# A hybrid decoder trunk on one core: first queries earlier in attention's lead-in, compressed items spread, background reordered

## The chip, the cores and the metric

The kernel runs on one core of a Trainium2 chip. The metric is the device time of one execution in microseconds (us); lower is better. Before the change the median of three runs is 1143.22 us (1142.72 to 1144.98).

## The reference

The reference is a small two-layer decoder over one sequence of 512 tokens with 1024 features, in float32. Layer 0 is a gated short convolution and a squared-ReLU MLP of width 4096. Its output feeds one shared key/value side. Layer 1 is attention with 16 heads of 64 in 4 key/value groups, then a second MLP, then a final norm.

Attention is what the change concerns. For each group, queries attend in three branches:

- a **compressed** branch, over 31 tokens that a small MLP (`phi`) makes out of overlapping blocks of 32 raw keys or values;
- a **selected** branch, over the best blocks (here all causal blocks are taken, since 16 may be chosen and only 8 exist);
- a **window** branch over 512 tokens, which is all of the causal past.

Each branch is a softmax with a learned relative-position bias; three sigmoid gates weigh them, and an output projection adds the result to the residual:

```python
o = gt[..., 0:1] * o_c + gt[..., 1:2] * o_s + gt[..., 2:3] * o_w
...
return o.reshape(B, S, N_HEADS * HEAD_DIM) @ w_o
```

## The kernel before

**Number format.** Each float32 operand of a product is split into two float16 parts, high and low, and a product is three matmuls: high by high, low by high, high by low (`mm3`, L338, issues L339 to L341). Weights come as float32 pieces over SyncE's DMA queue (`load_piece`, L155 to L165). ScalarE makes the high part (L193), VectorE the low part (L194). Pieces are taken in the order of one list, `pieces`, written at the head of the kernel (L70 to L130), and are converted two ahead of their use.

**Attention's lead-in** (L865) runs six generators to their ends, one after the other: `keys(0)`, `keys(1)`, `values(0)`, `values(1)`, `gates()`, `queries(0)`. Key and query generators each issue 48 matmuls of 128x512 through `gated_pair` (L651). `queries(g)` (L730) then scales two banks on VectorE (L643), copies four 64-row heads to float16 on ScalarE (L738) and subtracts to get the low half on GpSimd (L739). A query tile `Q` has three buffers.

**Attention's main loop** (L1089 to L1107) walks a list of items. `Full(g, qb, br, heads)` (L917) is one 128-row query block of one branch, with up to 512 columns; a group has 22 of them. `Cmp(gp, qb)` (L990) is a query block of the compressed branch, for two groups at once; there are 8. Each item has five stages, and the loop runs stage 0 of item i, then stage 1 of item i-2, stage 2 of item i-3, stage 3 of item i-4 and stage 4 of item i-6:

- stage 0: query-key matmuls into one of two `b` banks (L937, L938; L1005, L1006 for `Cmp`), bias and minimum on VectorE (L945), exponential on ScalarE (L947);
- stage 1: transposes (L953; L1026) and the high half of the probabilities on ScalarE (L956);
- stage 2: the low half, `at_pl`, on VectorE (L959; L1033);
- stage 3: probability-value matmuls (L972 to L974; L1042 to L1044), scaling and adding of branches (`add_parts`, L872; VectorE L890, GpSimd L892 and L895);
- stage 4: `finish` (L897) transposes a finished block (L906) into `ot`.

The order of items is all of group 0, all of group 1, the four `Cmp(0, qb)`, group 2, the four `Cmp(1, qb)`, group 3. The items are numbered 0 to 95 below, so the `Cmp` are items 44 to 47 and 70 to 73, and groups 2 and 3 begin at items 48 and 74.

**Background.** Other matrix work is drawn in between, from one generator `background()` (L1073). `raw(w)` (L746) projects raw keys or values, rescales them with a strided read on VectorE (L757) and gathers them through twelve small DMAs on SyncE's queue into `big` (L763 to L765). `phi(w)` (L771) is the compressing MLP, 96 matmuls of 155 columns over `big`, with a short chain of small operations behind them (L798). `out_proj(0)` (L841) is the output projection of groups 0 and 1. The order is raw 0, queries 1, phi 0, raw 1, phi 1, queries 2, queries 3, then `out_proj(0)` once groups 0 and 1 are finished ("o1"). Each yield tells a price; after each item's stage 0 a credit is added (1.1 for items under 44, then 0.7), and background is drawn until the credit is spent. An item whose queries or compressed keys aren't there yet (`need`) first draws background until they are; such a draw isn't charged. After the loop, `out_proj(2)`, for groups 2 and 3, runs by itself, and the second MLP follows.

The written order is then arranged for each engine by the framework's scheduler, which may move instructions of different work past each other; each engine runs its own list strictly in that order.

Of the kernel before, what the change touches and what calls it, by code (L numbers as in the profile page):

```python
# [48 lines left out]
def body(ctx, tc, x, rel_bias, norm_mix, norm_mlp, mlp_w1, mlp_w2, a_w_in, a_conv_w, a_w_out,  # L49
# [50 lines left out]
    def block(w, c0, scale=SW, k0=0, kn=8):  # L100
        for k in range(k0, k0 + kn, 4):
            cols(w, c0, 256, scale, k, 4)
# [8 lines left out]
    for p in range(4):  # L111
        block(a_w_out[0], p * 256)
    mlp_pieces(0)
    for part in (2, 4, 3, 5):
        block(w_kv, part * 256)
    cols(b_w_qg[0], 1024, 48, SW)
    block(b_w_qg[0], 0)
    block(w_kv, 0)
    block(b_w_qg[0], 256)
    block(phi_k_w1, 0, SW, 0, 16)  # L120
    cols(phi_k_w2, 0, 64, SW, 0, 2)
    block(w_kv, 256)
    block(phi_v_w1, 0, SW, 0, 16)
    cols(phi_v_w2, 0, 64, SW, 0, 2)
    block(b_w_qg[0], 512)
    block(b_w_qg[0], 768)
    for g in range(0, 4, 2):
        for p in range(4):
# [75 lines left out]
    def next_piece():  # L204

        i = pos["use"]
        pos["use"] += 1
        while i not in ready:
            for _ in convert_piece():
                pass  # L210
        return ready.pop(i)
# [177 lines left out]
    for p in range(4):  # L389
        pc, pu, pb = [], [], []  # L390
        if p == 0:
# [10 lines left out]
            for c in range(6):  # L402
                w = next_piece()
# [194 lines left out]
    with pool("attn") as ap:  # L598
# [70 lines left out]
        def ahead_fine():  # L669
            while pos["cv"] < min(pos["use"] + AHEAD, len(pieces)):  # L670
                yield from convert_piece(512)
# [57 lines left out]

        def queries(g):  # L730
            po = yield from gated_pair(xq)
            q = ap.tile([128, 4, S], F16, name="Q", bufs=3)
            for m in range(2):
                t = scaled(po[m], rbq)
                for s in range(2):
                    h, r = 2 * m + s, slice(64 * s, 64 * s + 64)
                    o = slice(64 - 64 * s, 128 - 64 * s)
                    ACT.activation(q[r, h], t[r], AF.Copy)  # L738
                    POOL.tensor_tensor(q[o, h], t[r], q[r, h], op=OP.subtract)  # L739
                yield  # L740
            Qs[g] = q
# [96 lines left out]
        ss2 = SumSq()  # L838
        xm = None

        def out_proj(g):  # L841
            for p in range(4):
                w = next_piece()
                cv = ahead_fine()
                po = [abank(), abank()]
                for c in range(4):
                    for m in range(2):
                        mm3(po[m], [u[:, c, m * 128:(m + 1) * 128] for u in w], [u[:, 2 * g + c] for u in ot],
                            c == 0, c == 3)
                        next(cv, None)  # L850
                        yield 0.65
                for m in range(2):
                    residual_in(po[m], 2 * p + m, 1.0 / (SO * SW))
                    if g == 2:
                        ss2.add(X[:, 2 * p + m])
                if g == 2:
                    for m in range(2):
                        split_gain(xm, 2 * p + m, X[:, 2 * p + m], "mlp1")
                drain(cv)
# [2 lines left out]
            yield from gen  # L862
            done.add(name)

        for k in (keys(0), keys(1), values(0), values(1), gates(), marked("q0", queries(0))):  # L865
            drain(k)
        lead_in[0] = False

# [121 lines left out]
        class Cmp:  # L990
# [7 lines left out]

            def st0(self):
                gp, qb, n = self.gp, self.qb, self.n  # L1000
                s = bank("b")[:, 0:256].rearrange("p (h n) -> p h n", h=8)
                for j in range(8):
                    g, h = 2 * gp + j // 4, j % 4
# [62 lines left out]
        def full(g):  # L1066
            return [Full(g, qb, br, hs) for qb in range(4) for br in range(2) for hs in heads_of(qb)]

        items = full(0) + full(1) + [Cmp(0, qb) for qb in range(4)] + full(2) + [Cmp(1, qb) for qb in range(4)]
        items += full(3)  # L1070
        at_item = {11: lambda: load_T(1), 35: lambda: load_T(2), 60: lambda: load_T(3)}

        def background():  # L1073
            yield from raw(0)
            yield from marked("q1", queries(1))
            yield from phi(0)
            yield from raw(1)
            yield from marked("cmp", phi(1))
            yield from marked("q2", queries(2))
            yield from marked("q3", queries(3))  # L1080
            while "o1" not in done:
                yield "wait"
            yield from out_proj(0)
# [1 line left out]
        bg = background()  # L1085

        lead = {1: 2, 2: 3, 3: 4, 4: 6}
        credit = 0.0
        for i in range(len(items) + 6):  # L1089
            if i < len(items):  # L1090
                for k in items[i].need():
                    while k not in done:
                        if next(bg, "end") in ("wait", "end"):
                            raise RuntimeError(k)
                at_item.get(i, lambda: None)()
                items[i].st0()
            credit += 1.1 if i < 44 else 0.7
            while credit > 0.0:
                u = next(bg, "end")
                if u in ("wait", "end"):  # L1100
                    credit = 0.0
                else:
                    credit -= u or 0.1
            for s in (1, 2, 3, 4):
                j = i - lead[s]
                if 0 <= j < len(items):
                    getattr(items[j], f"st{s}")()  # L1107
# [1 line left out]
            pass  # L1109
        lead_in[0] = True  # L1110
        xm = new_split(work, "xs")
        drain(out_proj(2))
    xs = xm
    ss = ss2

# [140 lines left out]
```

## Time and profile before

| what | value |
|---|---|
| median of three runs | 1143.22 us |
| profiled execution | 1147.34 us |
| its span, first to last instruction | 1145.5 us |
| matmul engine (PE) busy | 1102.9 us, 96% |
| VectorE (DVE) busy | 833.8 us, 73% |
| ScalarE (ACT) busy | 569.7 us, 50% |
| GpSimd (POOL) busy | 152.8 us, 13% |
| mean granted clock of the matmul engine | 0.987 |

The profile counts a matmul as busy from its start to the end of its pipeline, so matmuls that follow each other overlap, and a busy share near 100% doesn't mean that no time is lost. Two other readings tell more: the idle time before an instruction with the instruction that ended it (written in brackets in the timeline), and the clock that the matmul engine was granted (PEclk, 1.00 is full speed). The times in the timeline count from the start of the span. Attention lies between about 507 us (first key matmul) and 807 us (last matmul of the output projection); the rest of the program is convolution and MLPs.

### The profile page before, as it was taken

How to read it: one execution, taken by the hardware profiler on the slowest of the kernel's cores; microseconds unless marked ns; L12 is line 12 of the kernel's file. 1: busy time of each engine (PE TensorE's matmuls, PEld its weight loads, DVE VectorE, ACT ScalarE, POOL GpSimd, SP SyncE). 2: the span in 40 equal slices, each digit the busy share in tenths (PEclk: the TensorE clock that was granted, in tenths of full speed). 3: DMA queues.
4: the chain of work that ended last, by engine and by line, in shares of the span. 5: the costliest groups of instructions: out<-in, count | busy, mean ns of one | idle time of the engine just before them, and what ended most of it. 6: DMA issues, size and time to landing. Idle time of an engine off the chain costs nothing.

```text
span 1145.5 us, 20148 instructions
## 1 busy us (share of the span) xinstructions
PE 1102.9 (96%) x7959; PEld 695.8 (61%) x7959; DVE 833.8 (73%) x1504; ACT 569.7 (50%) x925; POOL 152.8 (13%) x201
## 2 busy tenths in 40 slices
PE   8999999999999999999999889999999999999986
PEld 4444444447884458868467566665444788445875
DVE  5755557865897557987489878897885598754785
ACT  4523235445333444457669656776554533343452
POOL 0000000322000220000102003221122100122020
PEclk9999999999999999999899999999999999999998
DMA  6423235433333333314234241101633333330221
GB/s 208 130 92 110 93 111 166 122 95 97 125 100 109 110 110 100 104 45 131 93 77 132 75 152 38 39 20 56 198 115 111 96 111 112 108 94 17 77 89 74
DMA packets 149378, 115.75 MB, mean 101 GB/s; under 512 B 8612, under 2 KB 146564, under 8 KB 149284
## 3 DMA queue, kind: packets, MB, share of 16 engines
q1 hardware_dynamic: 146736, 109.47, 31.6%
q10 hardware_dynamic: 2260, 4.40, 1.3%
q8 instruction: 62, 1.02, 0.4%
q0 software_dynamic: 288, 0.61, 0.2%
q14 instruction: 32, 0.26, 0.1%
HBM read 110.22 MB, written 2.14 MB: 98 GB/s over the span
## 4 chain that ended last, share of the span: by engine, by line
PE 58%; DVE 17%; ACT 8%; issue 6%; POOL 5%; DMA 4%; SPq 0%; DVEq 0%; ACTq 0%; POOLq 0%
PE a L339 5%; PE a L340 5%; PE a L341 5%; POOL ml_z L501 4%; DMA wst<-mlp_w_dram 4%; PE c L341 3%; PE c L339 3%; PE c L340 3%; PE b L340 3%; PE b L339 3%; DVE wlo L183 3%; PE b L341 3%; ACT rh L502 3%; PE c L953 2%; DVE wlo L194 2%
## 5 line engine op out<-in xcount | busy, mean ns | idle before, releaser
L193 ACT ACTIVATE whi<-wst 128x1024 f16<-128x1024 f32 (+2 forms) x171 | 141.9, 856 | 133.8 <-PE b L340 39.3
L194 DVE SCALAR_TENSOR_TENSOR wlo<-wst,whi 128x1024 f16<-128x1024 f32 (+2 forms) x171 | 168.6, 992 | 53.6 <-ACT whi L193 53.2
L501 POOL TENSOR_TENSOR ml_z<-ml_z 128x256 f32<-128x256 f32 x128 | 95.7, 769 | 609.7 <-ACT ml_z L499 607.1
L182 ACT ACTIVATE whi<-wst 128x1792 f16<-128x1792 f32 x64 | 106.7, 1691 | 135.5 <-DVE wst L180 107.3
L339 PEld LDWEIGHTS <-whi 128*128 128x128 f16 x1024 | 100.7, 98 | 112.3 <-issue 4.2
L341 PEld LDWEIGHTS <-wlo 128*128 128x128 f16 x1024 | 100.5, 98 | 110.9 <-issue 1.5
L340 PEld LDWEIGHTS <-whi 128*128 128x128 f16 x1024 | 100.5, 98 | 108.2 <-issue 3.5
L503 DVE TENSOR_TENSOR rl<-ml_z,rh 128x1792 f16<-128x1792 f32 x32 | 64.8, 2026 | 130.7 <-ACT rh L502 130.6
L183 DVE SCALAR_TENSOR_TENSOR wlo<-wst,whi 128x1792 f16<-128x1792 f32 x64 | 128.8, 2019 | 3.3 <-ACT whi L182 2.9
L180 DVE TENSOR_TENSOR wst<-wst 128x256 f32<-128x256 f32 x256 | 110.1, 473 | 28.0 <-DMA wst<-mlp_w_dram 27.0
L502 ACT ACTIVATE rh<-ml_z 128x1792 f16<-128x1792 f32 x32 | 54.3, 1697 | 100.9 <-POOL ml_z L501 100.9
L549 PEld LDWEIGHTS <-whi 128*128 128x128 f16 x896 | 87.9, 98 | 15.3 <-issue 4.5
L550 PEld LDWEIGHTS <-wlo 128*128 128x128 f16 x896 | 87.9, 98 | 12.1 <-DVE wlo L183 1.0
L548 PEld LDWEIGHTS <-whi 128*128 128x128 f16 x896 | 88.0, 98 | 10.8
L947 ACT ACTIVATE at_p<-at_s,at_m 128x128 f32<-128x128 f32 (+3 forms) x128 | 70.9, 555 | 20.8 <-DVE at_m L945 20.2
L499 ACT ACTIVATE ml_z<-ml_t 128x1024 f32<-128x1024 f32 x32 | 33.8, 1057 | 93.1 <-DVE ml_t L497 93.1
L341 PE MATMUL b<-xsh,wlo 128*128 128x512 f16 x208 | 78.8, 379 | 0.0
L340 PE MATMUL b<-xsl,whi 128*128 128x512 f16 x208 | 78.8, 379 | 0.0
L339 PE MATMUL b<-xsh,whi 128*128 128x512 f16 x208 | 78.7, 379 | 0.0
L341 PE MATMUL c<-xsh,wlo 128*128 128x512 f16 x192 | 73.5, 383 | 0.0
L339 PE MATMUL c<-xsh,whi 128*128 128x512 f16 x192 | 73.5, 383 | 0.0
L340 PE MATMUL c<-xsl,whi 128*128 128x512 f16 x192 | 73.3, 382 | 0.0
(312 smaller groups left out, 2690.6 us busy)
## 6 DMA issues: line engine op xcount, KB each, us to landing
wst<-mlp_w_dram SPq DMA_DIRECT2D x256, 256.0 KB, 3.3
wst<-a_w_in_dram SPq DMA_DIRECT2D x18, 512.0 KB, 3.6
wst<-w_kv_dram SPq DMA_DIRECT2D x12, 512.0 KB, 3.6
T<-ext_d ACTq DMA_DIRECT2D x4, 1056.0 KB, 6.7
wst<-a_w_out_dram SPq DMA_DIRECT2D x8, 512.0 KB, 3.3
wst<-b_w_qg_dram SPq DMA_DIRECT2D x8, 512.0 KB, 4.1
wst<-b_w_o_dram SPq DMA_DIRECT2D x8, 512.0 KB, 3.3
wst<-a_w_in_dram SPq DMA_DIRECT2D x8, 384.0 KB, 5.6
```

Source lines behind the costliest of these rows:

```text
L180: DVE.tensor_tensor(b[:, :, o], b[:, :, x], b[:, :, y], op=e)
L182: ACT.activation(hi, b[:, :, 1:], AF.Copy, scale=sc)
L183: DVE.scalar_tensor_tensor(lo, b[:, :, 1:], sc, hi, op0=OP.mult, op1=OP.subtract)
L193: ACT.activation(hi[:, s:e], w, AF.Copy, scale=sc)
L194: DVE.scalar_tensor_tensor(lo[:, s:e], w, sc, hi[:, s:e], op0=OP.mult, op1=OP.subtract)
L339: PE.matmul(ps, w[0], xs[0], start=start, stop=False)
L340: PE.matmul(ps, w[0], xs[1], start=False, stop=False)
L341: PE.matmul(ps, w[1], xs[0], start=False, stop=stop)
L501: POOL.tensor_tensor(z[:, o], z[:, a], z[:, b], op=e)
L502: ACT.activation(rh[0][:, p], z[:, 1:8], AF.Copy)
L548: PE.matmul(acc7[i], wh, xh, start=c == 0 and not other, stop=False, skip_group_check=other)
L549: PE.matmul(acc7[i], wh, xl, start=False, stop=False, skip_group_check=other)
```

## The change

The change touches attention and the list of weight pieces that goes with it. In the lead-in, `queries(0)` comes third, ahead of `values(0)`, `values(1)` and `gates()`. In the background, `queries(2)` stands ahead of `phi(1)`. `queries(3)` waits, once its matmuls are drawn, until stage 0 of `Cmp(0, 3)` has been issued ("cmp0"), since it reuses the buffer of `Q` of group 0. The compressed items no longer stand four in a row: `Cmp(0, qb)` go among the last 12 items of group 2 (items 54, 57, 60 and 63), and `Cmp(1, qb)` among those of group 3 (items 74, 79, 84 and 89). Groups 2 and 3 therefore begin at items 44 and 70. The credit starts at 3.0, and an item adds 0.91 (items under 54), 0.72 (under 68) or 0.6. At the end, `out_proj(2, 2)` first issues, for two of its four column pieces, the products that need group 2 alone. The arithmetic is the same.

```diff
@@ -111,18 +111,20 @@
     for p in range(4):
         block(a_w_out[0], p * 256)
     mlp_pieces(0)
-    for part in (2, 4, 3, 5):
+    for part in (2, 4):
+        block(w_kv, part * 256)
+    block(b_w_qg[0], 0)
+    for part in (3, 5):
         block(w_kv, part * 256)
     cols(b_w_qg[0], 1024, 48, SW)
-    block(b_w_qg[0], 0)
     block(w_kv, 0)
     block(b_w_qg[0], 256)
     block(phi_k_w1, 0, SW, 0, 16)
     cols(phi_k_w2, 0, 64, SW, 0, 2)
     block(w_kv, 256)
+    block(b_w_qg[0], 512)
     block(phi_v_w1, 0, SW, 0, 16)
     cols(phi_v_w2, 0, 64, SW, 0, 2)
-    block(b_w_qg[0], 512)
     block(b_w_qg[0], 768)
     for g in range(0, 4, 2):
         for p in range(4):
@@ -729,6 +731,8 @@
 
         def queries(g):
             po = yield from gated_pair(xq)
+            while g == 3 and "cmp0" not in done:
+                yield "wait"
             q = ap.tile([128, 4, S], F16, name="Q", bufs=3)
             for m in range(2):
                 t = scaled(po[m], rbq)
@@ -838,17 +842,29 @@
         ss2 = SumSq()
         xm = None
 
-        def out_proj(g):
-            for p in range(4):
-                w = next_piece()
-                cv = ahead_fine()
-                po = [abank(), abank()]
-                for c in range(4):
+        def out_proj(g, early=0):
+
+            ws, pos_ = [], []
+
+            def products(p, chunks, cv=iter(())):
+                for c in chunks:
                     for m in range(2):
-                        mm3(po[m], [u[:, c, m * 128:(m + 1) * 128] for u in w], [u[:, 2 * g + c] for u in ot],
-                            c == 0, c == 3)
+                        mm3(pos_[p][m], [u[:, c, m * 128:(m + 1) * 128] for u in ws[p]],
+                            [u[:, 2 * g + c] for u in ot], c == 0, c == 3)
                         next(cv, None)
                         yield 0.65
+
+            for p in range(early):
+                ws.append(next_piece())
+                pos_.append([abank(), abank()])
+                drain(products(p, (0, 1)))
+            for p in range(4):
+                if p >= early:
+                    ws.append(next_piece())
+                    pos_.append([abank(), abank()])
+                po = pos_[p]
+                cv = ahead_fine()
+                yield from products(p, (2, 3) if p < early else range(4), cv)
                 for m in range(2):
                     residual_in(po[m], 2 * p + m, 1.0 / (SO * SW))
                     if g == 2:
@@ -862,7 +878,7 @@
             yield from gen
             done.add(name)
 
-        for k in (keys(0), keys(1), values(0), values(1), gates(), marked("q0", queries(0))):
+        for k in (keys(0), keys(1), marked("q0", queries(0)), values(0), values(1), gates()):
             drain(k)
         lead_in[0] = False
 
@@ -998,6 +1014,8 @@
 
             def st0(self):
                 gp, qb, n = self.gp, self.qb, self.n
+                if (gp, qb) == (0, 3):
+                    done.add("cmp0")
                 s = bank("b")[:, 0:256].rearrange("p (h n) -> p h n", h=8)
                 for j in range(8):
                     g, h = 2 * gp + j // 4, j % 4
@@ -1066,8 +1084,18 @@
         def full(g):
             return [Full(g, qb, br, hs) for qb in range(4) for br in range(2) for hs in heads_of(qb)]
 
-        items = full(0) + full(1) + [Cmp(0, qb) for qb in range(4)] + full(2) + [Cmp(1, qb) for qb in range(4)]
-        items += full(3)
+
+        def mixed(rest, cmps):
+            out_ = []
+            for i, item in enumerate(rest):
+                out_.append(item)
+                if i in cmps:
+                    out_.append(cmps[i])
+            return out_
+
+        items = full(0) + full(1)
+        items += mixed(full(2), {9 + 2 * qb: Cmp(0, qb) for qb in range(4)})
+        items += mixed(full(3), {3: Cmp(1, 0), 7: Cmp(1, 1), 11: Cmp(1, 3), 15: Cmp(1, 2)})
         at_item = {11: lambda: load_T(1), 35: lambda: load_T(2), 60: lambda: load_T(3)}
 
         def background():
@@ -1075,8 +1103,8 @@
             yield from marked("q1", queries(1))
             yield from phi(0)
             yield from raw(1)
+            yield from marked("q2", queries(2))
             yield from marked("cmp", phi(1))
-            yield from marked("q2", queries(2))
             yield from marked("q3", queries(3))
             while "o1" not in done:
                 yield "wait"
@@ -1085,7 +1113,7 @@
         bg = background()
 
         lead = {1: 2, 2: 3, 3: 4, 4: 6}
-        credit = 0.0
+        credit = 3.0
         for i in range(len(items) + 6):
             if i < len(items):
                 for k in items[i].need():
@@ -1094,7 +1122,7 @@
                             raise RuntimeError(k)
                 at_item.get(i, lambda: None)()
                 items[i].st0()
-            credit += 1.1 if i < 44 else 0.7
+            credit += 0.91 if i < 54 else 0.72 if i < 68 else 0.6
             while credit > 0.0:
                 u = next(bg, "end")
                 if u in ("wait", "end"):
@@ -1109,7 +1137,7 @@
             pass
         lead_in[0] = True
         xm = new_split(work, "xs")
-        drain(out_proj(2))
+        drain(out_proj(2, 2))
     xs = xm
     ss = ss2
```

## The prediction

> **What bounds the kernel now.** I read the page's totals first, then a table of stretches over attention alone, since every edit lies there, then the list of waits of the matmul engine (PE), and last the timeline at the places that the waits name.
>
> ```profile
> span 1145.5 us, 20148 instructions
> ...
> PE 1102.9 (96%) x7959; PEld 695.8 (61%) x7959; DVE 833.8 (73%) x1504; ACT 569.7 (50%) x925; POOL 152.8 (13%) x201
> ```
>
> The profiled execution took 1147.34 us, 1.8 us more than its span; the median is 1143.22 us. The sum below is made against the profiled execution and its saving carried over to the median. By busy time PE is the bound, but busy counts matmuls to the end of their pipeline, so the share hides losses. The stretches show where they are (busy us per engine, then clock).
>
> ```profile
> core 0: us, PE busy (x) PEld busy (x) DVE busy (x) ACT busy (x) POOL busy (x), PEclk, DMA share, GB/s
> 507.00:557.00 50.00, 50.00 (x417) 33.63 (x416) 36.67 (x72) 32.18 (x61) 0.03 (x1) 1.00 0.43 133
> 557.00:567.40 10.40, 7.98 (x36) 3.59 (x35) 4.38 (x22) 7.39 (x24) 4.94 (x4) 0.67 0.17 53
> ...
> 590.00:622.00 32.00, 30.41 (x372) 23.71 (x369) 27.95 (x82) 27.26 (x79) 5.77 (x5) 1.00 0.47 132
> ...
> 642.70:659.70 17.00, 12.30 (x151) 8.43 (x149) 13.89 (x30) 10.28 (x24) 0.99 (x2) 0.90 0.40 94
> 659.70:694.00 34.30, 29.27 (x313) 20.15 (x314) 25.21 (x80) 19.15 (x50) 7.37 (x8) 0.95 0.40 125
> 694.00:730.00 36.00, 34.49 (x351) 24.23 (x349) 31.79 (x88) 29.62 (x84) 11.03 (x10) 1.00 0.14 45
> 730.00:785.00 55.00, 54.57 (x635) 38.96 (x634) 53.28 (x165) 42.43 (x119) 9.16 (x14) 1.00 0.10 30
> 785.00:807.30 22.30, 21.27 (x143) 10.60 (x142) 15.72 (x28) 11.88 (x21) 2.52 (x4) 1.00 0.24 72
> ```
>
> Three stretches are bad: 557 to 567.4, 642.7 to 659.7 and 659.7 to 694. Each has idle PE and a granted clock under 1.00. From 694 on PE and VectorE (53.28 of 55) are both nearly full, so little is to be had there. The waits name the causes (us in total, times, longest).
>
> ```profile
> PE b L937 <- POOL Q L739: 5.8, 9, 1.0
> PE c L953 <- DVE at_pl L959: 4.0, 4, 1.8
> PE a L339 <- DVE phi_t L798: 1.8, 1, 1.8
> ...
> PE c L906 <- POOL o L895: 0.9, 1, 0.9
> ```
>
> The matmul engine's full-speed pace, needed to price work, comes from the starts of neighbours:
>
> ```profile
> 571.73 0.38 PE L339 MATMUL a<-xsh,whi 128*128 128x512 f16 x1
> 571.94 0.38 PE L340 MATMUL a<-xsl,whi 128*128 128x512 f16 x1
> ...
> 634.37 0.49 PE L953 MATMUL c<-ident,at_p 128*128 128x128 f32 x3
> 634.69 0.19 PE L972 MATMUL d<-VT,at_ph 128*128 128x64 f16 x1
> 634.72 0.19 PE L973 MATMUL d<-VT,at_ph 128*128 128x64 f16 x1
> ```
>
> So 0.215 us for 512 columns (narrower ones in proportion), 0.107 for a transpose (0.32 for three), 0.03 for a probability-value product.
>
> **Part 1: queries 0 third in the lead-in.** Today the lead-in ends with queries 0, and the first items need them at once.
>
> ```profile
> 556.95 0.38 PE L339 MATMUL a<-xsh,whi 128*128 128x512 f16 x1
> 558.22 0.23 PE L937 MATMUL b<-KD,Q 128*128 128x128 f16 x1 [0.89 <-POOL Q L739]
> ...
> 563.05 0.63 PE L339 MATMUL a<-xsh,whi 128*128 128x512 f16 x1
> 563.48 0.63 PE L340 MATMUL a<-xsl,whi 128*128 128x512 f16 x1
> ...
> 567.32 0.28 PE L953 MATMUL c<-ident,at_p 128*128 128x128 f32 x1
> ```
>
> From 556.95 to 567.32 pass 10.37 us. In them PE starts 14 matmuls of 512 columns, 4 of 256 and 16 of 128, worth 14 x 0.215 + 4 x 0.107 + 16 x 0.054 = 4.3 us. So 6.0 us are lost: waits for the four GpSimd subtractions, and half speed after them (563.05 to 563.48 is 0.43 for a matmul). In the new order 192 matmuls of `values` and 96 of `gates` stand between queries 0 and the first item, some 23 us, against 5.2 us of GpSimd work (below). The wait goes whole. Next late is the first item's `b` bank, which `values(1)` now holds until VectorE has emptied it, while the gates' 2.6 us of matmuls cover most. I take a gain of **5.0**, bounds 3.5 and 6.0. In the lead-in itself the same pieces are converted at the same rate and PE loses nothing today (50.00 of 50.00), with VectorE at 36.67; I cost it at nothing, at worst 2.
>
> GpSimd's subtractions now run beside VectorE work in the lead-in instead of beside a waiting PE.
>
> ```profile
> 556.47 0.68 DVE L194 SCALAR_TENSOR_TENSOR wlo<-wst,whi 128x512 f16<-128x512 f32 x1
> 556.97 5.20 POOL L739 TENSOR_TENSOR Q<-at_s,Q 64x512 f16<-64x512 f32 x4 [119.35 <-ACT Q L738]
> 559.48 1.68 DVE L194 SCALAR_TENSOR_TENSOR wlo<-wst,whi 128x512 f16<-128x512 f32 x1 [2.34 <-ACT whi L193]
> ```
>
> The same VectorE operation takes 0.68 us at 556.47 and 1.68 beside a subtraction: 1.0 us more. The Trainium skill, SBUF — State Buffer, in its rules of contention, says that a VectorE instruction with two SBUF inputs and a GpSimd one that reads SBUF exclude each other; the trace agrees, with that 1.0 us. In the lead-in VectorE has 13 us free, so I add nothing; where VectorE is full, it is rival 2.
>
> **Part 2: queries 2 between raw 1 and phi 1.** Today phi 1 follows raw 1 and waits for its gather:
>
> ```profile
> 640.22 0.38 PE L341 MATMUL a<-xsh,wlo 128*128 128x512 f16 x1
> ...
> 642.35 1.94 DVE L757 TENSOR_TENSOR at_s<-a,rb 128x512 f32<-128x512 f32 x2
> ...
> 657.75 0.61 SPq L765 DMA_DIRECT2D big<-kr_hl  x1
> ...
> 659.70 0.23 PE L339 MATMUL a<-big,whi 128*128 128x155 f16 x1 [0.77 <-issue]
> ```
>
> The last raw matmul ends its turn at 640.4, phi 1 begins at 659.70: 19.3 us, with VectorE's strided pair (which also holds up `at_pl`: 1.8 us of PE) and twelve DMAs on SyncE in a row. In that gap only items run. The stretch 642.7 to 659.7 loses 17.00 - 12.30 = 4.7 us idle and 0.10 x 17.0 = 1.7 to the clock, 6.4 together. In the changed program's written order the gap holds all 48 matmuls of queries 2, 26 transposes, 66 probability products and 10 score matmuls of 512: 48 x 0.215 + 26 x 0.107 + 66 x 0.03 + 10 x 0.215 = 17.2 us. That is 2.1 short of 19.3, so phi 1 may still wait a little. I take **5.0**, bounds 2.5 and 6.4. SyncE's weight loads for queries 2 stand ahead of phi's now; they are two of the same size and swap places, so I cost them at nothing; a late one would show inside the bounds.
>
> Behind phi 1, today, queries 3's predecessor in the same two `a` banks waits 1.8 us for `phi_t`. In the new order 3 transposes, 12 products and 3 score matmuls or so stand there, about 1.3 us. Gain **1.5**, bounds 0.5 and 1.8.
>
> **Part 3: the hand-over of queries 2.** Group 2 begins at item 44, not 48. The credit by then is 3.0 + 44 x 0.91 = 43.0; queries 2 end at 10.6 (raw 0) + 10.6 + 7.2 + 10.6 + 10.6 = 49.6. So 6.6 are drawn by force, and in the written order 27 of queries 2's 48 matmuls do stand in one block, as today:
>
> ```profile
> 682.45 0.38 PE L341 MATMUL a<-xqh,wlo 128*128 128x512 f16 x1
> ...
> 691.35 0.29 PE L937 MATMUL b<-KD,Q 128*128 128x128 f16 x1 [0.22 <-POOL Q L739]
> ```
> ```profile
> PE b L937 <- POOL Q L739: 2.4, 4, 1.0
> ...
> PE a L339 <- DVE at_s L643: 0.7, 1, 0.7
> ```
>
> Today this costs 2.4 + 0.7 and 0.05 x 34.3 = 1.7 of clock, 4.8. The new order has 4 transposes, 12 phi products and 4 small ones, some 1.4 us, ahead of the first score of group 2, and 5.2 us of GpSimd after it as before: the same stall. **0**, bounds -1.5 and +1.5 (phi 1's shortfall of 2.1 falls into it, not onto it).
>
> **Part 4: compressed items spread, queries 3, the pause.** The 8 `Cmp` issue what they did. Queries 3 now end by credit at item 65 or 66, four ahead of their need, and "o1" comes at item 69, so items 66 to 69 have no background. VectorE's share of such an item, from its rows:
>
> ```profile
> L959 DVE SCALAR_TENSOR_TENSOR at_pl<-c,at_ph 128x512 f16<-128x512 f32 x26 | 17.7, 686 | 1.5 <-ACT at_ph L956 1.4
> L945 DVE CUSTOM_DVE_ANT_0 at_s<-b,T 128x512 f32<-128x512 f32 x16 | 10.9, 684 | 2.3 <-POOL Q L739 2.0 <-PE b L938 0.3
> ```
>
> 0.69 + 0.68 and small ones, about 1.6 us, against PE's 2 x 0.215 + 4 x 0.107 + 12 x 0.03 = 1.2: four items lose 1.6 us of PE. I take **-1.5**, bounds -4 (queries 3's 5.2 us of subtractions uncovered) and 0. The rates 0.91, 0.72 and 0.6 move the same background about within stretches where PE is full: 0, bounds -1.5 and +1.
>
> **Part 5: early products.** They can stand ahead of the last `finish`, whose 0.9 us wait is in the list. The scheduler already moves some there. **+0.5**, bounds 0 and 0.9.
>
> **Sum:** 5.0 + 5.0 + 1.5 + 0 - 1.5 + 0.5 = 10.5 us. The profiled execution would take 1136.8, the median 1143.2 - 10.5 = **1132.7 us**.
>
> **Rivals.**
>
> Rival 1, slower: the clock. PE's lost time turns into half speed; 557 to 567.4 lost (1 - 0.67) x 10.4 = 3.4 us so. If the thinner cover (0.6 instead of 0.7, none in items 66 to 69) lets the small waits of groups 2 and 3 do this, each such event takes 3.4. It decides from four events: 4 x 3.4 = 13.6, more than 10.5 by 3.1, 1146 us. For it: three stretches cool today. Against: 694 to 785 has 1.00 with a like cover. Chance 4%. The Trainium skill, TensorE: Matmul & The Clock Gate, in its part on the clock gate, puts the halving down to a free-running window of about 3.4 us with too little work; 3.4 and 1.7 us lost at half speed are 6.8 and 3.4 us of time, two such windows and one, so the trace agrees. By it each stall that is left may cost 1.7 us more or less than today, as its place in the window falls.
>
> Rival 2, little gain: VectorE bounds from item 44 on. What PE saves ahead of it, VectorE makes up for, since spread `Cmp` put some 0.3 us operations between full items' and GpSimd's subtractions for queries 3 hold it up to 4 x 1.0. Only part 1 stays, less 4: 1142. For it: 53.28 of 55. Against: 25.21 of 34.30 and 13.89 of 17.00 just where the gain lies. Chance 7%.
>
> Rival 3, more gain: hand-overs of queries 2 vanish behind VectorE's own queue, the first half loses nothing at 590 to 622 (30.41 of 32.00) and all upper bounds hold: 6.0 + 6.4 + 1.8 + 1.5 + 1 + 0.9 = 17.6, 1125.6 us. Chance 11%.
>
> Rival 4: the draws by force leave the order as it was, beyond the lead-in: 5 us, 1138 us. The written order speaks against it, as queries 2 do fill the gap. Chance 8%; it lies in the range.
>
> **How the numbers follow.** The forecast's mechanism with its bounds (6 to 17 us less) has 70%, rival 1 4%, rival 2 7%, rival 3 11%, rival 4 8%. The range 1125.5 to 1141.0 takes in the forecast and about half of rival 3. A measurement of this kernel tells 0.2% (2.3 us) from no change, so faster means under 1140.9. Faster: 70, 11 and 8, 89%, and a little of rival 2: 0.90. Same: most of rival 2: 0.05. Slower: rival 1 and an unforeseen 1%: 0.05.
>
> **What would show it.** In the changed profile the clock over the first items should be 1.00 and the first L937 wait for no `Q`; the gap between raw 1 and phi 1 should hold `xq` matmuls with no 1.8 us wait at L953; `Q` waits should be left at group 2 alone, near 3 us; DVE should stay near 97% in group 3. If `Q` waits at group 3 exceed 3 us, or PE cools there, part 4 is wrong; if the first items still cool, part 1 is.

## The result and the profile after

| kernel | median us (lowest to highest, runs) | ratio to before, 95% interval |
|---|---|---|
| before, run beside it | 1144.65 (1142.72 to 1145.96, 6) | 1 |
| changed kernel | 1138.12 (1136.88 to 1139.53, 6) | 0.9945 [0.9935, 0.9956] |

The change gains 6.5 us where 10.5 were forecast. Curiously, the two profiled executions differ by just the forecast sum: 1147.34 against 1136.88 us, 10.5 us. One lay 2.7 us over its kernel's median and the other 1.2 under, so that agreement is worth little by itself; the first experiment comes back to it.

In the changed kernel the lines of attention are shifted: the product helper L339 to L341 is L341 to L343, the query subtraction L739 is L743, scores L937 and L938 are L953 and L954, the bias and minimum L945 is L961, transposes L953 are L969, `at_pl` L959 is L975, the finished block's L906 is L922, the GpSimd sum L895 is L911. First the page's totals:

```profile
span 1135.1 us, 20099 instructions
...
PE 1095.8 (97%) x7959; PEld 694.1 (61%) x7959; DVE 832.3 (73%) x1498; ACT 568.5 (50%) x922; POOL 157.6 (14%) x198
```

Busy time says next to nothing again: PE went from 96% to 97%. The table of stretches of the changed kernel says more (stretch and length, busy us of PE, weight loads, VectorE, ScalarE, GpSimd, then granted clock):

```profile
507.00:555.00 48.00, 48.00 (x404) 32.60 (x402) 37.37 (x67) 30.51 (x57) 6.06 (x4) 1.00 0.37 113
555.00:567.00 12.00, 12.00 (x100) 7.70 (x97) 7.81 (x39) 11.96 (x38) 0.00 (x0) 1.00 0.40 129
...
641.00:658.60 17.60, 15.23 (x119) 8.41 (x119) 13.36 (x28) 10.65 (x23) 1.57 (x2) 1.00 0.60 149
658.60:694.00 35.40, 33.25 (x462) 26.51 (x463) 29.96 (x104) 29.23 (x91) 7.42 (x10) 1.00 0.24 79
694.00:710.00 16.00, 15.02 (x160) 10.18 (x157) 15.22 (x41) 10.95 (x26) 6.18 (x6) 1.00 0.10 34
710.00:720.00 10.00, 7.13 (x81) 6.02 (x80) 8.00 (x23) 6.86 (x17) 4.76 (x5) 0.83 0.01 2
720.00:766.00 46.00, 45.43 (x519) 32.53 (x516) 44.78 (x137) 34.30 (x99) 8.09 (x11) 1.00 0.15 47
```

The three bad stretches of before are better: 555 to 567, where the first items run now, has no idle PE; the stretch between raw 1 and phi 1 has 15.23 of 17.60 (before 12.30 of 17.00); the one behind it 33.25 of 35.40 (before 29.27 of 34.30). All three have clock 1.00. But a new bad one has come: 710 to 720, the first items of group 3, with 7.13 of 10.00 and a clock of 0.83. The list of PE's waits in attention (us in total, times, longest) names what is left:

```profile
PE b L953 <- POOL Q L743: 2.5, 5, 0.6
PE b L953 <- DVE at_m L961: 2.1, 3, 1.2
PE a L341 <- DMA big<-kr_hl: 2.1, 1, 2.1
PE c L969 <- DVE at_pl L975: 2.0, 4, 1.0
PE c L922 <- POOL o L911: 1.5, 2, 0.9
PE e L312 <- DVE rs_r L305: 0.9, 1, 0.9
```

The `Q` waits fell from 5.8 to 2.5, the `phi_t` wait of 1.8 is off the list, `at_pl` halved. Others grew: the wait for `o` from 0.9 to 1.5, and the wait for VectorE's `at_m`, which frees a `b` bank, from what stood here before:

```profile
PE b L937 <- DVE at_m L945: 1.2, 3, 0.5
```

The waits for the gather into `big` and for the next MLP's norm (`rs_r`) are new in the list. The first, 2.1 us, is the shortfall that the prediction worked out (17.2 of 19.3 us filled), and it stands just there in the timeline:

```profile
658.57 0.23 PE L341 MATMUL a<-big,whi 128*128 128x155 f16 x1 [2.06 <-DMA big<-kr_hl]
...
660.46 0.23 PE L953 MATMUL b<-KD,Q 128*128 128x128 f16 x1 [0.16 <-POOL Q L743]
...
661.68 0.23 PE L953 MATMUL b<-KD,Q 128*128 128x128 f16 x1 [0.56 <-POOL Q L743]
...
662.91 0.23 PE L953 MATMUL b<-KD,Q 128*128 128x128 f16 x1 [0.62 <-POOL Q L743]
...
705.70 0.38 PE L343 MATMUL a<-xqh,wlo 128*128 128x512 f16 x1
...
708.10 0.66 PE L969 MATMUL c<-ident,at_p 128*128 128x128 f32 x4
...
712.04 0.38 PE L953 MATMUL b<-KD,Q 128*128 128x512 f16 x1 [1.25 <-DVE at_m L961]
...
713.77 0.23 PE L953 MATMUL b<-KD,Q 128*128 128x128 f16 x1 [0.49 <-POOL Q L743]
...
715.09 1.09 PE L969 MATMUL c<-ident,at_p 128*128 128x128 f32 x4 [1.03 <-DVE at_pl L975]
...
720.72 0.59 PE L341 MATMUL a<-big,whi 128*128 128x512 f16 x2 [0.34 <-ACT big L362]
```

Behind it come the three waits that are left of the hand-over of queries 2, 1.3 us in all. The longest wait for `at_m`, 1.25 us at 712.04, begins a row of three that makes the bad stretch (1.25, 0.49 and 1.03 us, 2.8 together). Then PE runs at half speed: a group of four transposes takes 1.09 us at 715.09, for 0.66 at 708.10. The whole bad stretch lies where PE has no background: between the last product of queries 3 at 705.70 and the first of the output projection at 720.72 it starts no background matmul for 15.0 us.

### The profile page after: what moved, and what is told of

Same layout as the page of the kernel before. It is cut to its first block, busy times and chain, and to the rows that moved or that the text cites. A ratio compares the mean times of both kernels' runs of the same rounds, so it can differ in the third digit from the quotient of the medians.

```text
span 1135.1 us, 20099 instructions
## 1 busy us (share of the span) xinstructions
PE 1095.8 (97%) x7959; PEld 694.1 (61%) x7959; DVE 832.3 (73%) x1498; ACT 568.5 (50%) x922; POOL 157.6 (14%) x198
## 4 chain that ended last, share of the span: by engine, by line
PE 50%; DVE 19%; ACT 11%; issue 7%; POOL 7%; DMA 5%; SPq 1%; DVEq 0%; ACTq 0%; POOLq 0%
POOL ml_z L503 6%; PE a L341 4%; PE a L342 4%; PE a L343 4%; DVE wlo L185 4%; DMA wst<-mlp_w_dram 3%; ACT rh L504 3%; PE c L343 3%; PE c L342 3%; PE c L341 3%; PE b L342 3%; PE b L341 3%; PE b L343 3%; DVE wlo L196 3%; DVE ml_t L499 2%
## 5 line engine op out<-in xcount | busy, mean ns | idle before, releaser
L195 ACT ACTIVATE whi<-wst 128x1024 f16<-128x1024 f32 (+4 forms) x171 | 142.4, 858 | 127.9 <-PE b L342 38.4
L196 DVE SCALAR_TENSOR_TENSOR wlo<-wst,whi 128x1024 f16<-128x1024 f32 (+4 forms) x171 | 169.9, 1001 | 40.2 <-ACT whi L195 39.9
L503 POOL TENSOR_TENSOR ml_z<-ml_z 128x256 f32<-128x256 f32 x128 | 99.9, 801 | 610.1 <-ACT ml_z L501 410.1
L341 PEld LDWEIGHTS <-whi 128*128 128x128 f16 x1024 | 100.4, 98 | 112.3 <-issue 5.5
L343 PEld LDWEIGHTS <-wlo 128*128 128x128 f16 x1024 | 100.2, 98 | 112.1 <-issue 0.4
L550 PEld LDWEIGHTS <-whi 128*128 128x128 f16 x896 | 87.7, 98 | 10.5
L343 PE MATMUL b<-xsh,wlo 128*128 128x512 f16 x208 | 78.8, 379 | 0.0
L341 PE MATMUL b<-xsh,whi 128*128 128x512 f16 x208 | 78.7, 379 | 0.0
L551 PE MATMUL a<-rl,whi 128*128 128x256 f16 x256 | 69.8, 273 | 3.7 <-DVE rl L505 3.7
L341 PE MATMUL c<-xsh,whi 128*128 128x512 f16 x192 | 72.8, 379 | 0.0
```

The source lines that it names most:

```text
L195: ACT.activation(hi[:, s:e], w, AF.Copy, scale=sc)
L196: DVE.scalar_tensor_tensor(lo[:, s:e], w, sc, hi[:, s:e], op0=OP.mult, op1=OP.subtract)
L341: PE.matmul(ps, w[0], xs[0], start=start, stop=False)
L343: PE.matmul(ps, w[1], xs[0], start=False, stop=stop)
L503: POOL.tensor_tensor(z[:, o], z[:, a], z[:, b], op=e)
L550: PE.matmul(acc7[i], wh, xh, start=c == 0 and not other, stop=False, skip_group_check=other)
```

## The experiments

All ratios are to the kernel before, timed on the same chip.

**Before, once more.** No edit. The question was how much of what the forecast took from one execution is that execution's own.

> The kernel before, unchanged, to learn how its runs differ among themselves. The profiled execution of before was 1147.3 us at a mean clock of 0.987, 2.7 us over its median; the changed kernel's was 1136.9 at 0.995, 1.2 under its median. Theory A, the profiled pair overstates the gain because half-speed stretches fall differently from run to run: clocks from 0.987 to about 0.992 over the runs, with the time following the clock, about 1.7 us for each 0.0015. Theory B, the clock is the same in every run and the spread is something else: 0.987 throughout with times between 1143 and 1146.

Measured: 1144.57 us (1142.13 to 1148.92, 12 runs), ratio 1.0002 [0.9990, 1.0014]. Its profile was the surprise. Two of the stretches that had clocks of 0.67 and 0.95 in the first profile, and the waits for `Q` from 550 to 570 (the first profile's, then this one's):

```profile
556.50:567.00 10.50, 7.66 (x56) 4.54 (x54) 5.87 (x29) 8.28 (x26) 4.97 (x4) 1.00 0.17 51
...
660.00:694.00 34.00, 28.48 (x293) 18.76 (x291) 28.39 (x91) 22.40 (x66) 9.32 (x10) 1.00 0.40 124
```
```profile
PE b L937 <- POOL Q L739: 2.4, 4, 0.9
```
```profile
PE b L937 <- POOL Q L739: 2.8, 4, 0.9
```

PE waits for the four subtractions again (2.8 us here, 2.4 in the first profile), but the clock stays at 1.00; and from 660 to 694 it is idle for 5.5 us, more than the 5.0 of the first profile, again at 1.00. In this whole execution attention has no half-speed stretch, where the first profile had three (6.8, 3.4 and 3.4 us long). So like waits cool the clock in one execution and not in another. The Trainium skill, TensorE: Matmul & The Clock Gate, in its part on the clock gate, calls the window free-running and the cold time variable from run to run; these two executions agree with that.

To weigh the parts I therefore add up, matmul by matmul, the time from one start to the next less the pace of that shape (0.216 us for 512 columns, 0.056 for 128, 0.109 for a transpose), by stretches that count from the first key matmul. In brackets stands half the length of the half-speed stretches, which is what they can have cost at most:

| PE time lost, us (half speed) | 0 to 95 | 95 to 190 | 190 to 260 | 260 to 325 | sum |
|---|---|---|---|---|---|
| before, first profile | 8.1 (3.4) | 19.2 (3.4) | 3.9 | 5.2 | 36.4 |
| before, once more | 5.9 | 17.8 | 3.9 | 4.9 | 32.4 |
| lead-in alone | 1.6 | 19.7 (3.4) | 3.8 | 4.7 | 29.9 |
| changed kernel | 1.9 | 11.5 | 8.9 (1.7) | 3.5 | 25.8 |
| changed, no early products | 1.9 | 11.1 | 8.4 | 2.7 | 24.1 |

From the second before to the changed kernel 6.6 us go, and the medians differ by 6.5. The table shows what the sum hides: 4.0 saved in the lead-in and first items, 6.3 from there past the hand-over to group 2, **5.0 lost again** around group 3, and 1.4 saved at the end.

**The lead-in alone.** The kernel before with queries 0 third and their pieces moved with them.

```diff
-        for k in (keys(0), keys(1), values(0), values(1), gates(), marked("q0", queries(0))):
+        for k in (keys(0), keys(1), marked("q0", queries(0)), values(0), values(1), gates()):
```

> Before with the first edit alone: queries 0 third in the lead-in, with its weight pieces moved to match. Theory A, the hand-over of queries 0 was worth its price of 5 us and nothing takes its place: about 1139.5 us, ratio 0.9955, clock 1.00 over the first items. Theory B, the gain is mostly given back, as VectorE and ScalarE carry into the first items what queries 0 left behind: 1142 to 1143, ratio 0.998.

Measured: 1138.71 us (1137.69 to 1141.23, 6 runs), ratio 0.9949 [0.9936, 0.9963]: 5.9 us. The stretch of the first items is full:

```profile
556.00:568.00 12.00, 12.00 (x99) 7.81 (x95) 8.12 (x42) 11.96 (x41) 0.00 (x0) 1.00 0.25 83
```

The longest that are left in its list of waits are what parts 2 and 3 set out to remove:

```profile
PE c L955 <- DVE at_pl L961: 4.4, 4, 1.8
PE b L939 <- POOL Q L741: 3.7, 5, 1.0
PE a L341 <- DVE phi_t L800: 1.8, 1, 1.8
```

**All but the lead-in.** The changed kernel with that line and its pieces as before.

> The changed kernel with the first edit undone (queries 0 last in the lead-in again). Theory A, the terms add up: 5 us slower than the changed kernel, about 1143 us, ratio 0.999, so that everything else in the change is worth only 1.5 us. Theory B, the rest of the change is worth more and the terms overlap: 1140, ratio 0.996.

Measured: 1143.72 us (1141.55 to 1145.97, 11 runs), ratio 0.9988 [0.9976, 0.9999]. All the rest, most of the diff, is worth 0.9 us together, though several of its waits did go. The next runs ask why.

**A shorter pause.** `Cmp(0, qb)` closer together, so that "cmp0" and "o1" come earlier and items 66 to 69 have background.

```diff
-        items += mixed(full(2), {9 + 2 * qb: Cmp(0, qb) for qb in range(4)})
...
+        items += mixed(full(2), {9 + qb: Cmp(0, qb) for qb in range(4)})
```

They are items 54, 56, 58 and 60 then.

> The changed kernel with the four compressed items of groups 0 and 1 at every other place (items 54, 56, 58, 60 instead of 54, 57, 60, 63). Groups 0 and 1 are then finished three items earlier, at item 66, when queries 3 are drawn, and the output projection can follow without a pause. Theory A, the pause without background at items 66 to 69 is what costs at 700 to 720 us (clock 0.83 and PE 7.13 of 10 there): 3 us less than the changed kernel, about 1135, ratio 0.992. Theory B, it is the GpSimd subtractions of queries 3 that group 3 waits for, whatever stands beside: 1138, ratio 0.9945, with waits for Q as long as before.

Measured: 1138.10 us (1137.51 to 1139.63, 5 runs), ratio 0.9943 [0.9930, 0.9955]: nothing. The time in which PE starts no background matmul fell from 15.0 us to 7.2 (706.44 to 713.59), so the edit halves the pause and doesn't remove it. From 706 to 720 PE stays idle about as long, now at clock 1.00, beside a fuller VectorE (the changed kernel first, then this one):

```profile
706.00:720.00 14.00, 10.73 (x120) 8.15 (x119) 11.59 (x33) 10.55 (x26) 7.16 (x6) 0.88 0.01 2
```
```profile
706.00:720.00 14.00, 10.44 (x113) 7.03 (x112) 13.06 (x28) 10.88 (x25) 7.27 (x6) 1.00 0.12 39
```

The loss stays under other names, in its list of waits from 705 to 770:

```profile
PE a L342 <- DVE big L364: 1.4, 1, 1.4
PE d L988 <- DVE o_t L906: 1.1, 2, 0.7
PE c L922 <- DVE at_pl L975: 0.9, 2, 0.7
PE d L988 <- ACT at_ph L972: 0.7, 1, 0.7
PE b L953 <- DVE at_m L961: 0.6, 1, 0.6
```

All but one are waits for VectorE. That turned the question to what bounds group 3.

**Less PE work, less VectorE work.** Two kernels that leave work out of group 3, the second out of group 2 as well. In the first `out_proj(0)` makes one of its three products (64 matmuls fewer, 64 x 0.216 = 13.8 us of PE):

```diff
-                        mm3(pos_[p][m], [u[:, c, m * 128:(m + 1) * 128] for u in ws[p]],
-                            [u[:, 2 * g + c] for u in ot], c == 0, c == 3)
+                        if g == 0:
+                            PE.matmul(pos_[p][m], ws[p][0][:, c, m * 128:(m + 1) * 128], ot[0][:, 2 * g + c],
+                                      start=c == 0, stop=c == 3)
...
```

> Leaves work out: the output projection of groups 0 and 1, which is the background from item 70 on, issues one of its three products per tile, 64 matmuls of 512 columns fewer, 64 x 0.215 = 13.8 us of the matmul engine. Theory A (the forecast's: PE bounds groups 2 and 3): 11 to 14 us less than the changed kernel, 1125 to 1127. Theory B (rival 2: VectorE bounds from item 44 on): under 5 us less, 1134 or more.

In the second the full items of groups 2 and 3 make no low half of their probabilities. The products with it are left out too, 160 matmuls of 0.03 us, so that up to 4.8 us of PE go as well (the expectation reckoned with half as many):

```diff
+                if self.g >= 2:
+                    return
```

> Leaves work out: the full items of groups 2 and 3 make no low half of the probabilities, and issue no product with it. That takes 44 VectorE operations of 0.55 to 0.69 us, about 28 us, off VectorE, and about 80 x 0.03 = 2.4 us off the matmul engine. Theory A (PE bounds groups 2 and 3): 2 to 5 us less than the changed kernel, 1133 to 1136. Theory B (VectorE bounds): the time falls until PE bounds, by 8 us or more, 1130 or less.

Measured: 1133.61 us (1131.89 to 1135.58, 4 runs), ratio 0.9904 [0.9887, 0.9921], 4.5 us for 13.8 us of PE work less; and 1127.51 us (1126.90 to 1128.52, 4 runs), ratio 0.9848 [0.9831, 0.9865], 10.6 us for VectorE work (and those products) less. The rows of group 3 in the changed kernel, then with less PE work, then with less VectorE work (PE is the first busy figure, VectorE the third):

```profile
712.50:766.00 53.50, 51.31 (x588) 37.78 (x587) 51.58 (x156) 38.72 (x109) 10.52 (x13) 0.97 0.13 41
```
```profile
712.50:766.00 53.50, 46.71 (x546) 34.74 (x545) 50.60 (x156) 39.66 (x111) 9.84 (x14) 0.94 0.10 31
```
```profile
712.50:758.50 46.00, 45.78 (x500) 33.87 (x498) 38.31 (x127) 38.22 (x108) 9.89 (x13) 1.00 0.12 36
```

With less PE work group 3's scores run from 713.3 to 765.0, 51.7 us, for 52.9 in the changed kernel (712.7 to 765.6): PE stands idle, and cools, while VectorE is busy 50.60 of 53.50. By the trace, 44 of the 64 matmuls, 9.5 us, were missing from this stretch, and by the count of lost time 18.5 us go from 190 to 260 for 8.9: the work that was taken out there turned into waiting. The 4.5 us gained are about the other 20 matmuls (4.3 us), which stood behind group 3's scores. With less VectorE work the scores run from 712.6 to 758.2, 45.6 us, and PE is full at clock 1.00. **So VectorE bounds group 3 as soon as PE has less to do there.** In the kernel before both engines were about as full, and no run tells which of them set the length. The four `Cmp(1)` and group 3 in its first profile:

```profile
733.00:741.60 8.60, 8.60 (x158) 6.86 (x157) 8.60 (x30) 5.63 (x14) 0.61 (x3) 1.00 0.20 63
741.60:781.30 39.70, 39.29 (x413) 27.66 (x409) 38.53 (x125) 31.80 (x95) 8.54 (x11) 1.00 0.10 28
```

That is 48.3 us with 47.1 of VectorE work; the same items now lie in 53.5 us with 51.6. The 4.5 us more aren't the background's; the largest growth is in the low halves of probabilities, 16 of 128x512 for 13 before, 2.1 us. The background's two large groups on VectorE, the weights' low halves and the additions into `X`, come to 10.2 us in those 48.3 us of before and to 9.5 us in the 53.5 of the changed kernel (busy us and mean ns of one):

```profile
L467 DVE SCALAR_TENSOR_TENSOR X<-a,X 128x512 f32<-128x512 f32 x8 | 5.4, 678 | 0.0
L194 DVE SCALAR_TENSOR_TENSOR wlo<-wst,whi 128x512 f16<-128x512 f32 x7 | 4.8, 679 | 0.0
```
```profile
L196 DVE SCALAR_TENSOR_TENSOR wlo<-wst,whi 128x512 f16<-128x512 f32 x8 | 5.5, 683 | 0.0
...
L469 DVE SCALAR_TENSOR_TENSOR X<-a,X 128x512 f32<-128x512 f32 x6 | 4.0, 682 | 0.0
```

Nor does the lost time lie where VectorE is full. By the rows of the changed kernel PE is idle for 0.57 us from 720 to 766, with VectorE busy 44.78 of 46; from 710 to 720, with VectorE busy 8.00 of 10, it is idle for 2.87 us and loses up to 1.7 to half speed. So the new loss stands at the hand-over to group 3, where there is no background. A full VectorE leaves little room behind that place, and with the shorter pause little room in it.

**That work on GpSimd.** If those 5.5 us of weights' low halves could go to the idle engine, the stretch should shrink. Two kernels, without early products, do it from item 46 and from item 70:

```diff
+                if on_pool[0] and n == 256:
+                    POOL.tensor_scalar(w, w, sc, None, op0=OP.mult)
+                    POOL.tensor_tensor(lo[:, s:e], w, hi[:, s:e], op=OP.subtract)
+                else:
+                    DVE.scalar_tensor_tensor(lo[:, s:e], w, sc, hi[:, s:e], op0=OP.mult, op1=OP.subtract)
```

> The changed kernel without early products, and with the low halves of the weights made by GpSimd (a scaling and a subtraction) instead of VectorE for all pieces converted during items 46 to 95. It takes some 24 operations of 0.69 us, 16 us, off VectorE in the stretch that it bounds by theory B, and puts about 2.5 us apiece on GpSimd, which was idle over half of it. Theory A (VectorE bounds there, and one relieved operation in two or three shows): 4 to 8 us less than the 1136.4 us without early products, 1129 to 1132. Theory B (the low halves come too late for the products, or GpSimd's queue holds up Q and the sums): 1137 or more, with waits for wlo or Q.

> The same, but only from item 70 on, behind the subtractions of queries 3, so that GpSimd's queue can't hold up Q. About 10 VectorE operations, 7 us, are taken away. Theory A: 2 to 4 us less than 1136.4, 1132 to 1134. Theory B: 1137 or more. If this is faster and the other is not, GpSimd's queue is what decides the other.

Measured: 1231.05 us, ratio 1.0750 [1.0732, 1.0767], and 1226.04 us, ratio 1.0704 [1.0686, 1.0723], four runs each. They reach further than meant: the work stays on GpSimd into the second MLP, where some 80 of the 90 to 95 us are lost. In attention itself the second gains nothing either: its last matmul starts 296.1 us after the first key matmul, for 289.3 without the edit. GpSimd is slow at it (128x512 pieces):

```profile
L198 POOL TENSOR_SCALAR wst<-wst 128x512 f32<-128x512 f32 x16 | 25.1, 1578 | 8.2 <-ACT whi L196 8.0
...
L199 POOL TENSOR_TENSOR wlo<-wst,whi 128x512 f16<-128x512 f32 x16 | 18.5, 1165 | 0.7
```

1.58 + 1.17 = 2.7 us for a piece that VectorE does in 0.68. And from item 70 on wasn't late enough: two such pieces run on GpSimd from 711.06 to 716.24, between the subtractions of queries 3, and PE waits for those:

```profile
PE b L958 <- POOL Q L748: 5.5, 2, 4.6
```

So GpSimd's queue did hold up `Q`, and these two runs don't tell what a relieved VectorE would be worth.

**No draws by force.** Higher rates at first, so that queries 2 are done before group 2 asks for them.

```diff
-            credit += 0.91 if i < 54 else 0.72 if i < 68 else 0.6
+            credit += 1.06 if i < 44 else 0.8 if i < 68 else 0.6
```

> The changed kernel with the credits 1.06 (items under 44), 0.8 (under 68) and 0.6, so that queries 2 are drawn before group 2 begins and not by force. Theory A, what is left to gain at item 44 is the 2.1 us wait of phi 1 for its DMAs and 2.5 us of waits for Q: 2 to 3 us less than the changed kernel, 1135.5. Theory B, VectorE bounds the second half, and what is saved at item 44 comes back as waits for VectorE: 1138, ratio 0.9945.

Measured: 1145.35 us (1142.94 to 1148.79, 12 runs), ratio 1.0007 [0.9996, 1.0018], 7 us over the changed kernel. This change of two rates costs as much as the whole change gains. In its waits `at_m` is worse than in the changed kernel (2.6 us for 2.1), and the longest wait for `Q` is 1.6 us for 0.6:

```profile
PE b L953 <- DVE at_m L961: 2.6, 3, 1.3
PE b L953 <- POOL Q L743: 2.3, 4, 1.6
```

By the count of lost time its profiled execution loses 31.0 us for 25.8, of which 2.8 more from 95 to 190 (with up to 3.4 of half speed there, behind the 1.6 us wait for queries 2). The rest of the 7 us is not accounted for.

**Part 2 with the old rates.** The lead-in, queries 2 ahead of phi 1, and `Cmp(0)` among group 2, with the credits of before (0.0 at first, then 1.1 and 0.7), `Cmp(1)` four in a row and no early products.

```diff
-            yield from marked("cmp", phi(1))
             yield from marked("q2", queries(2))
+            yield from marked("cmp", phi(1))
```

> The lead-in edit, queries 2 between raw 1 and phi 1 and the compressed items of groups 0 and 1 among group 2, but the old credits (0 at first, 1.1 and 0.7), the compressed items of groups 2 and 3 four in a row as before, and no early products. Against the lead-in edit alone (1138.7) this is part 2 with what it needs. Theory A (part 2 is worth its 5 us, and the new rates and the pause lose it again): 1133 to 1135. Theory B (VectorE bounds from item 44 on, so that part 2 can't pay whatever the rates): 1137 to 1139.

Measured: 1141.23 us (1138.94 to 1146.14, 12 runs), ratio 0.9967 [0.9954, 0.9980], 2.5 us slower than the lead-in alone, though the two intervals overlap. Its profiled execution was the slowest of the twelve (1146.14 us), so its rows show more loss than the median has. The gap between raw 1 and phi 1 is full:

```profile
640.00:660.00 20.00, 19.89 (x188) 12.79 (x187) 16.32 (x39) 12.90 (x30) 1.24 (x2) 1.00 0.45 108
714.00:724.00 10.00, 4.78 (x74) 4.34 (x74) 5.78 (x16) 5.83 (x13) 6.07 (x6) 0.75 0.01 2
```
```profile
718.63 0.18 PE L1023 MATMUL b<-KC,Q 128*128 128x8 f16 x1 [3.37 <-POOL Q L743]
```

Queries 3, held back until "cmp0", now end right ahead of `Cmp(1, 0)`, and PE stands still for GpSimd's subtractions: 4.78 of 10.00 at 0.75. In this execution what part 2 saves at queries 2 is paid at queries 3.

**No early products**, by itself and together with the closer compressed items.

```diff
-        drain(out_proj(2, 2))
+        drain(out_proj(2))
```

> The changed kernel without the early products of the last output projection. Theory A, part 5 is worth its 0.5 us: 1138.6, too small to tell from the changed kernel's 1138.1. Theory B, it is worth nothing or harms, as the last transposes still wait 0.9 us for GpSimd in the changed profile: 1138 or a little under. Either way under 1 us, which says that the missing microseconds aren't here; a loss of 2 us or more would speak against both.

> The changed kernel without its early output products, and with the four compressed items of head group 0 at every second of four places of group 2 (54, 56, 58, 60), so that the pause of four items at 66 to 69 is gone as well: the two edits that were run apart, together. Theory A (the early products cost about 1.7 us, the place of the compressed items nothing): 1136.4 us, ratio 0.993. Theory B (the 1.7 us were chance, neither edit matters): 1138.1 us, ratio 0.9945. Theory C (with the early products gone the pause shows: its stall of 2 us at 712 was covered by them): 1134.5 us, ratio 0.991.

| median us, ratio | with early products | without |
|---|---|---|
| `Cmp(0)` as changed | 1138.12, 0.9945 [0.9935, 0.9956] | 1136.42, 0.9931 [0.9918, 0.9945] |
| `Cmp(0)` closer | 1138.10, 0.9943 [0.9930, 0.9955] | 1136.85, 0.9936 [0.9922, 0.9949] |

Across, 1.7 and 1.25 us; downward nothing. In each pair the intervals overlap, but both pairs say the same. So the early products bring no gain and probably cost about 1.5 us. With `Cmp(0)` as changed the last wait for `o` is 0.9 with and without them, with `Cmp(0)` closer 1.2 with and without, so they don't cover it. The next MLP's wait for its norm is longer with them (0.9 us in the list above). Without:

```profile
PE c L922 <- POOL o L911: 0.9, 1, 0.9
PE e L312 <- DVE rs_r L305: 0.3, 1, 0.3
```

With the closer items it is 1.6 with them and 0.5 without.

The early loop is drained without `ahead_fine`, so the conversion of the next weights starts later; that this is the reason was only argued. 1136.42 us without early products is the lowest median of all kernels that leave no work out, 8.9 us under the kernel before timed beside it, though the intervals don't part it from the changed kernel.

## Why the prediction was partly right

The sign and the range held; the size was off by 4.0 us of gain (6.5 for 10.5), and 1.4 us more of the forecast's 5.4 came from the base: the median of before is 1144.65 over six runs, not 1143.22.

**Part 1** (+5.0, up to 6.0) was right in mechanism: no `Q` wait and clock 1.00 over the first items, 5.9 us by itself. Its size isn't settled to the microsecond. In the profiles the first 95 us lose 4.0 us less than in the second execution of before and 6.2 less than in the first, which cooled there. The lead-in itself cost nothing: PE is 48.00 of 48.00.

**Parts 2 and 3** (+5.0, +1.5, 0) were right in the sum. Between 95 and 190 the loss fell from 17.8 to 11.5, that is 6.3 for 6.5. The shortfall of 2.1 came as 2.06. But it didn't fall into part 3's stall as forecast: it stands ahead of phi 1 and counts in full, while the `Q` waits of group 2 came out smaller than "the same stall" (1.3 us for 2.4, at clock 1.00). Matmuls of phi 1 lay between those scores.

**Part 4** (-1.5, bounds -4 and 0) is the step that failed: its price of the pause. From 190 to 260 the loss rose from 3.9 to 8.9 us, 5.0 for 1.5, past the bound of 4. The place was right, and the prediction's own sign of an error there, PE cooling at group 3, came. It priced the four items without background by busy time alone, 1.6 us of VectorE against 1.2 of PE for each. What the changed profile shows instead are waits in a row, with no background matmul for 15.0 us to fill them: 1.25 us for `at_m`, 0.49 for `Q`, 1.03 for `at_pl`, and up to 1.7 us of half speed behind them, 4.5 together. The half speed matters little: the profile without early products has none there and still loses 8.4 us.

Why a pause half as long gained nothing is not shown. With it VectorE was busy 13.06 us of the 14 around the hand-over, so VectorE is the likely cause; no run took its work out of this place alone. Rival 2 was thus wrong in reach (1142: all but part 1 lost, and 4 more), and its mechanism shows in the runs with less work, but not as the cause of the 5.0 us. The prediction's other term here, rates at 0, holds in one respect, since the background asks VectorE for no more in group 3 than before (9.5 us for 10.2); but the run with higher rates shows that rates aren't free, at 7 us.

**Part 5** (+0.5) had the wrong sign, probably -1.5. The wait for `o` that they should have covered is unchanged.

**The base.** The terms were read off one execution with 13.6 us of half-speed stretches in attention (6.8, 3.4, 3.4), while another of the same kernel has none and loses 32.4 instead of 36.4 us. Stalls priced with their half speed (part 1's 3.4, part 2's 1.7) were priced too high for the median.

**Rivals.** Rival 1 (the clock) fell: one new stretch, not four. Rival 3 fell with part 4. Rival 4 named the measured time, 1138, by another cause: the order did change beyond the lead-in, and its gain was lost again, so the agreement is chance.

## What to carry to other kernels

Before background work is moved, list the stretches that are left without any, and price each by the waits that nothing covers then, not by busy time alone: here 15 us without background went with a loss of 4.5 us where 1.5 had been reckoned. List also which engine is full in each stretch: where PE and VectorE both are, work taken off PE turned into waiting. When a change has several parts, run the main part alone and the rest alone: here one reordered line was 5.9 of 6.5 us. A saving read off one profiled execution should have its half-speed time taken out, or be read off two.

## What the runs showed of the hardware

- Four waits for `Q` of at most 0.9 us each, 2.4 us together, went with 6.8 us at half clock in one execution of the kernel before, and four of 2.8 us together with none in the next. Attention, with 13.6 us of half speed in the first, lost 4.0 us more there.
- GpSimd took 1.58 us to scale a 128x512 float32 tile and 1.17 us for a subtraction to float16, against VectorE's 0.68 us for both in one instruction. The Trainium skill, GPSIMD Engine Reference, under performance versus the Vector engine, gives about 2.6 cycles at 1.2 GHz per element for two inputs, by which a 512-element row is an estimated 1.11 us; the subtraction agrees. Its best case of 1.8 cycles, an estimated 0.77 us, is half of what the scaling took here.
- Taking about 9.5 us of PE work out of a stretch in which PE was busy 51.31 of 53.50 us, and VectorE 51.58, shortened its scores only from 52.9 us to 51.7: PE waited then, beside a VectorE busy 50.60 of 53.50.
- Two conversions on GpSimd, 5.2 us, that ran between two subtractions for `Q` went with a wait of PE for `Q` of 4.6 us.
